# FFN input projections by Strassen's seven products on two of three token blocks, in a phase of their own

## The chip, the cores and the metric

The kernel runs on one core of a Trainium2 chip. The metric is the device time of one execution in microseconds (us). A profiled execution gives the trace from which all rows below are taken.

## The reference

The program is one step of a two-layer encoder over 1088 tokens (1024 of a new stream, 64 of a running one), with 1024 channels. Each layer is a mixer and a gated FFN, both behind an RMSNorm and with a residual sum. The change concerns the FFN alone:

```python
def conv_ffn(h, st, w_in, conv_w, conv_b, w_out):      # D_FF = 2816
    gu = h @ w_in
    g, u = gu[..., :D_FF], gu[..., D_FF:]
    g, new_st = causal_dwconv(g, conv_w, conv_b, st)   # width 3, along the tokens
    return (jax.nn.gelu(g) * u) @ w_out, new_st
# per layer: x = x + f, with f from conv_ffn(rmsnorm(x, norm_ffn[l]), ...)
```

## The kernel before

**Tiles.** Channels lie on the 128 partitions and tokens along the free axis: a tile is [128, T] with T = 1092, in three token blocks of BL = 364 (the text calls them blocks 0, 1 and 2). D_MODEL is KT = 8 such tiles, D_FF is FT = 22. Every fp32 operand is held as two fp32r parts h and l whose sum it is, and a product of a weight tile with an operand tile is three matmuls for each block: wh·xh, wl·xh and wh·xl (`product`, L167). One matmul has 128x128 weights and 364 columns. A projection of one output tile is thus 8 k-tiles x 3 terms x 3 blocks = 72 matmuls into one PSUM tile `pm` of three banks; the pool has two such tiles.

**Weights.** `weights` loads a [128, 1024] tile as two raw halves by SP's queue; ACT makes h by a copy (L131) and DVE makes l by a subtraction (L132).

**The FFN.** For each of the 22 tiles, `make` projects the gate (72 matmuls), multiplies it by 1/rms (L608), runs the conv (ACT L234, two DVE steps L236), GELU (ACT L611) and a product (L612); it then projects the up half (72 matmuls), multiplies it with the gate (L615), and splits the result into h and l in the pool `ring` (L186, L187). `chunks` runs the output product two k-tiles at a time, one step behind the making: `chunk` makes 8 output tiles of 18 matmuls each, and L260 adds each from PSUM to the residual sum XR, which stays in SBUF in eight slots of the pool `xr`. Input and output products alternate within the FFN.

**Before an FFN.** At the last chunk of the mixer's output product, `Next` makes the FFN's operands for each finished tile m: ACT L192 and DVE L193 scale and split it, and POOL adds its square to the sum for the norm (L202).

**What sets the order.** The Tile framework's scheduler orders each engine's instructions ahead of time by its own costs; on the chip each engine runs its list in that order, and waits at the first instruction whose semaphores are not there. Slots of a pool are reused in turn, so a new tile waits for the last reader of the tile before it.

Line numbers of this part are those of the kernel before; those named in the section on the change are of the changed one.

## Time and profile before

| what | value |
|---|---|
| three runs | 2795.62, 2793.54, 2795.61 us |
| median | 2795.61 us |
| span of the profiled execution | 2790.8 us |
| profiled execution beside the median | 4.8 us shorter |
| matmuls on PE | 16642, busy 98% of the span |
| DVE, ACT, POOL busy | 57%, 29%, 9% |

The span is the time from the first to the last instruction in the trace. Sums of durations are to be set against it, and the 4.8 us between it and the median of the three runs are carried along. The page shows shares of the whole span; the stretches show where one engine stands and another does not. PE stands for TensorE's matmuls, DVE for VectorE, ACT for ScalarE, POOL for GpSimd, and SP for the engine that issues most loads.

### The profile page before, as it was taken

The numbers are of one execution on the slowest core, as the hardware profiler recorded it, in microseconds if no ns is written. First come the engines' busy times: TensorE is split into PE (matmuls) and PEld (weight loads), VectorE is DVE, ScalarE is ACT, GpSimd is POOL, SyncE is SP. The second block draws the span as 40 slices with busy tenths as digits, with TensorE's granted clock in tenths as the row PEclk, the third lists the DMA queues.
The fourth block names the chain that finished last, engine by engine and source line by source line (L and its number), as shares of the span: only waits on it lengthen the run. The fifth ranks groups of instructions, "written<-read, shape, count | busy, mean of one in ns | idle before, by whom it ended". The sixth has DMA issues, their size and how long they took to land.

```text
span 2790.8 us, 39161 instructions
## 1 busy us (share of the span) xinstructions
PE 2745.5 (98%) x16642; PEld 2717.2 (97%) x16642; DVE 1601.7 (57%) x1723; ACT 803.4 (29%) x1083; POOL 242.8 (9%) x524
## 2 busy tenths in 40 slices
PE   8999999999999999999999999999999999999998
PEld 8999999999989999999999989999899999999997
DVE  7655665568675444444444587786744444444446
ACT  7323322232132222212212245551412112212223
POOL 1101111010030000000000030020300000000003
PEclk9999999999999999999999999999999999999999
DMA  3222332244211111111111121151111111111111
GB/s 131 78 82 81 99 97 82 86 127 138 66 43 41 46 46 46 42 46 42 46 46 45 64 82 58 55 199 53 38 46 46 42 46 45 42 46 42 42 47 68
DMA packets 83103, 183.02 MB, mean 66 GB/s; under 512 B 9808, under 2 KB 12416, under 8 KB 82928
## 3 DMA queue, kind: packets, MB, share of 16 engines
q1 hardware_dynamic: 67248, 123.40, 14.5%
q0 software_dynamic: 15392, 56.69, 6.1%
q8 instruction: 131, 2.15, 0.3%
...
## 4 chain that ended last, share of the span: by engine, by line
PE 94%; DVE 3%; issue 1%; ACT 1%; DMA 0%; POOL 0%; SPq 0%; DVEq 0%; ACTq 0%; POOLq 0%
PE pm L167 90%; DVE xg L193 1%; PE pa L507 1%; DVE xr L260 1%; PE pa L480 1%; PE pm L743 1%; DVE xg L772 0%; PE pa L518 0%; DVE wl L132 0%; PE pm L327 0%; PE pa L210 0%; PE pa L465 0%; DMA xr<-x 0%; DMA o_keep_lru<-keep_lru 0%; ACT xg L747 0%
## 5 line engine op out<-in xcount | busy, mean ns | idle before, releaser
L167 PE MATMUL pm<-xg,wh 128*128 128x364 f32 x7104 | 1406.8, 330 | 0.0
L167 PEld LDWEIGHTS pm<-xg,wh 128*128 128x128 f32 x7104 | 1204.6, 188 | 5.8 <-issue 2.6
L167 PE MATMUL pm<-xg,wl 128*128 128x364 f32 x3552 | 783.7, 328 | 0.0
L131 ACT ACTIVATE wh<-raw 128x512 fp32r<-128x512 f32 x440 | 274.8, 628 | 1481.7 <-PE pm L167 1259.8
L167 PE MATMUL pm<-ring,wh 128*128 128x364 f32 x3360 | 662.6, 331 | 22.3 <-DVE xr L260 17.2
L167 PEld LDWEIGHTS pm<-xg,wl 128*128 128x128 f32 x3552 | 619.9, 188 | 1.1
L167 PEld LDWEIGHTS pm<-ring,wh 128*128 128x128 f32 x3360 | 573.5, 189 | 27.4 <-DVE xr L260 20.2
L260 DVE TENSOR_TENSOR xr<-xr,pm 128x1092 f32<-128x1092 f32 x264 | 340.2, 1290 | 210.2 <-PE pm L167 204.4
L132 DVE TENSOR_TENSOR wl<-raw,wh 128x512 fp32r<-128x512 f32 x440 | 310.5, 708 | 243.8 <-ACT wh L131 243.6
L167 PE MATMUL pm<-ring,wl 128*128 128x364 f32 x1680 | 373.7, 331 | 0.0
L167 PEld LDWEIGHTS pm<-ring,wl 128*128 128x128 f32 x1680 | 295.4, 189 | 0.1
L226 POOL COPY wk<-par 128x2 f32<-128x2 f32 (+1 forms) x72 | 40.0, 555 | 1709.8 <-DVE wk L608 1416.2
L236 DVE SCALAR_TENSOR_TENSOR wk<-wk,par,wk 128x1092 f32<-128x1092 f32 x104 | 140.8, 1354 | 63.3 <-ACT wk L234 61.8
L608 DVE TENSOR_TENSOR wk<-pm,ss 128x1092 f32<-128x1092 f32 x44 | 57.0, 1295 | 193.0 <-PE pm L167 192.8
L615 DVE TENSOR_TENSOR wk<-pm,wk 128x1092 f32<-128x1092 f32 x44 | 57.0, 1295 | 119.7 <-PE pm L167 119.7
L187 DVE TENSOR_TENSOR ring<-wk,ring 128x1092 fp32r<-128x1092 f32 x68 | 87.9, 1294 | 36.5 <-ACT ring L186 32.8
L186 ACT ACTIVATE ring<-wk 128x1092 fp32r<-128x1092 f32 x68 | 75.7, 1116 | 100.0 <-PE pm L167 65.4
L612 DVE TENSOR_TENSOR wk<-wk,ss 128x1092 f32<-128x1092 f32 x44 | 57.0, 1296 | 52.1 <-ACT wk L611 52.1
L234 ACT ACTIVATE wk<-wk,par 128x1092 f32<-128x1092 f32 x52 | 67.7, 1302 | 65.5 <-POOL wk L226 65.3
L611 ACT ACTIVATE wk<-wk 128x1092 f32<-128x1092 f32 x44 | 49.2, 1118 | 121.2 <-DVE wk L236 121.2
L202 POOL TENSOR_TENSOR ss<-ss,wk 128x1092 f32<-128x1092 f32 x21 | 64.7, 3082 | 172.5 <-ACT wk L201 172.0
L193 DVE SCALAR_TENSOR_TENSOR xg<-xr,par,xg 128x1092 fp32r<-128x1092 f32 x32 | 64.5, 2024 | 11.8 <-ACT xg L192 11.5
...
## 6 DMA issues: line engine op xcount, KB each, us to landing
...
ring<-at_d POOLq DMA_DIRECT2D x16, 546.0 KB, 6.0
...
xr<-x SPq DMA_DIRECT2D x8, 546.0 KB, 7.3
...
```

Of the source, the lines that this page charges most:

```text
L131: S.activation(h, raw, AF.Copy)
L132: V.tensor_sub(l, raw, h.bitcast(F))
L167: TE.matmul(ps[:, b, 0:BL], w, x[:, b * BL:(b + 1) * BL], start=i == 0, stop=i == n - 1)
L186: S.activation(h, src, AF.Copy)
L187: V.tensor_sub(l, src, h.bitcast(F))
L193: split_last[0] = V.scalar_tensor_tensor(l, src, scale, h.bitcast(F), op0=OP.mult, op1=OP.subtract).ins
L202: by.tensor_add(ss, ss, sq)
L234: S.activation(out, cb[:, at:at + T], AF.Identity, bias=col(kind + "_b", i), scale=col(kind + "_w", i * w))
L236: V.scalar_tensor_tensor(out, cb[:, at + k:at + k + T], col(kind + "_w", i * w + k), out, op0=OP.mult, op1=OP.add)
L260: V.tensor_add(b3(XR[m]), b3(XR[m]), ps[:, :, 0:BL])
L608: V.tensor_mul(b3(cb[:, PAD:]), ps, b3(RS))
L612: V.tensor_mul(g, g, RS)
```

## The change

The gate and up projections are made for two output tiles at a time. The operand is a 2x2 block matrix: the two halves of the 8 k-tiles (k and k+4) by the token blocks 0 and 1. For these two blocks, `seven` makes seven products of half the depth in place of eight; block 2 is done plainly. Per pair of output tiles that is 7 x 12 + 2 x 24 = 132 matmuls, where before there were 2 x 72 = 144. One group is a pair's gate or a pair's up half: 22 groups in each layer.

`Pairs` takes the place of `Next` before an FFN. From each pair of residual tiles (m, m+4) it makes nine half-operands: `b11`, `b21`, `b22`, the combinations `t1` to `t4`, and `k0`, `k1` for the plain block. These fill 24 slots of `xg`. The order of the output tiles becomes 0, 4, 1, 5, 2, 6, 3, 7. `seven_weights` makes four weight operands from two raw tiles, among them two combinations: per group four ACT copies of 1024 columns (L348), four DVE subtractions of 1024 (L349) and four DVE steps of 512 (L353, L354, L357, L358). They fill the eight slots of `ring`.

In `seven`, `held` copies a product out of PSUM by ACT (L383), since it is needed by two sums or its bank is used again. `put` adds a held copy to a product (L740 in a gate group, L759 in an up group, 364 columns each), and at the second block multiplies 728 columns (L743 by 1/rms, L761 by the gate). `plain` evicts block 2 (L751, L765).

The results no longer go into the output product at once. Each is stored to DRAM (L762), all 22 groups of the layer come first, and then `chunks` reloads the tiles (L791) and splits them. `ring` is full of weights meanwhile, so the residual sum is also stored to DRAM and reloaded into `ring` (L710). All these transfers are issued by POOL. The pool `xg` has 24 slots instead of 16 and serves as `xr` as well; `raw` has two slots of 1024 columns instead of three of 512.

The core of the diff:

```diff
-    def xg(dt=R):
-        return slot("xg", 16, dt)
+    def xg(dt=R, cols=T):
+        return slot("xg", 24, dt, cols)
     def xr(dt=F, cols=T):
-        return slot("xr", 8, dt, cols)
+        return xg(dt, cols)
...
+    class Pairs(Next):
+        order = [m for k in range(HK) for m in (k, k + HK)]
+        def operands(self, m):
+            if m < HK:
+                return
+            x0, x1 = self.XR[m - HK], self.XR[m]
+            w0, w1 = col(self.key, m - HK), col(self.key, m)
+            ts, tu = wk(), wk()
+            u, t4 = tu[:, B[0]], tu[:, B[1]]
+            h, l = zip(*[(xg(), xg()) for _ in range(3)])
+            def scaled(i, b, n, x, w, at):
+                to = slice(b * BL, (b + n) * BL)
+                S.activation(h[i][:, to], x[:, at], AF.Copy, scale=w)
+                V.scalar_tensor_tensor(l[i][:, to], x[:, at], w, h[i][:, to].bitcast(F), op0=OP.mult, op1=OP.subtract)
+            S.activation(u, x0[:, B[0]], AF.Copy, scale=w0)
+            V.scalar_tensor_tensor(ts[:, B[0]], x0[:, B[1]], w0, u, op0=OP.mult, op1=OP.subtract)
+            V.scalar_tensor_tensor(ts[:, B[1]], x1[:, B[1]], w1, ts[:, B[0]], op0=OP.mult, op1=OP.subtract)
+            V.scalar_tensor_tensor(t4, x1[:, B[0]], w1, ts[:, B[1]], op0=OP.mult, op1=OP.subtract)
+            V.tensor_sub(ts[:, B[2]], ts[:, B[1]], u)
+            S.activation(h[2][:, B[0]], t4, AF.Copy)
+            V.tensor_sub(l[2][:, B[0]], t4, h[2][:, B[0]].bitcast(F))
+            scaled(2, 1, 1, x0, w0, B[2])
+            scaled(2, 2, 1, x1, w1, B[2])
+            S.activation(h[1], ts, AF.Copy)
+            V.tensor_sub(l[1], ts, h[1].bitcast(F))
+            scaled(0, 0, 1, x0, w0, B[0])
+            scaled(0, 1, 2, x1, w1, slice(0, 2 * BL))
+            self.xs.append((h, l))
+        def part(self, name, k):
+            i, b = PLACE[name]
+            h, l = self.xs[k]
+            return h[i][:, B[b]], l[i][:, B[b]]
+    def seven_weights(key0, key1):
...
+        out = []
+        raws = []
+        for key in (key0, key1):
+            n = n_of["w"] = n_of.get("w", 0) + 1
+            raw = wp.tile([P, 1024], F, tag="raw", bufs=2, name=f"raw{n}")
+            nc.sync.dma_start(raw, a[key[0]][key[1:]])
+            raws.append(raw)
+        r0, r1 = raws
+        lo, hi = slice(0, 512), slice(512, 1024)
+        def ready(raw):
+            h, l = ring(R, 1024), ring(R, 1024)
+            S.activation(h, raw, AF.Copy)
+            V.tensor_sub(l, raw, h.bitcast(F))
+            out.append((h, l))
+        ready(r1)
+        V.tensor_add(r1[:, hi], r1[:, lo], r1[:, hi])
+        V.tensor_sub(r1[:, lo], r0[:, lo], r1[:, lo])
+        ready(r1)
+        ready(r0)
+        V.tensor_sub(r0[:, lo], r1[:, hi], r0[:, lo])
+        V.tensor_sub(r0[:, hi], r0[:, hi], r0[:, lo])
+        ready(r0)
+        return out
...
+    def seven(ws, X, put, plain):
+        ta, tb = psum(), psum()
+        pw, pv1, pv0 = ta[:, 0, 0:BL], ta[:, 1, 0:BL], ta[:, 2, 0:BL]
+        px, py, pz = tb[:, 0, 0:BL], tb[:, 1, 0:BL], tb[:, 2, 0:BL]
+        def mul(ps, terms, first=True):
+            n = len(terms) * HK * 3
+            i = 0
+            for w, half, name in terms:
+                for k in range(HK):
+                    at = slice((half * HK + k) * P, (half * HK + k + 1) * P)
+                    wh, wl = w[0][:, at], w[1][:, at]
+                    xh, xl = X.part(name, k)
+                    for wx, x in ((wh, xh), (wl, xh), (wh, xl)):
+                        TE.matmul(ps, wx, x, start=first and i == 0, stop=i == n - 1, skip_group_check=True)
+                        i += 1
+        def held(ps):
+            n = n_of["cp"] = n_of.get("cp", 0) + 1
+            t = wp.tile([P, BL], F, tag="wh", bufs=6, name=f"cp{n}")
+            S.activation(t, ps, AF.Copy)
+            return t
+        a2, s31, a1, s24 = ws
+        mul(pw, [(a2, 1, "t4")])
+        mul(pv1, [(a2, 0, "k0"), (a2, 1, "k1")])
+        w = held(pw)
+        mul(pz, [(s31, 1, "t1")])
+        plain(1, pv1)
+        mul(px, [(a1, 0, "b11")])
+        p5 = held(pz)
+        mul(pv0, [(a1, 0, "k0"), (a1, 1, "k1")])
+        p1 = held(px)
+        mul(py, [(a1, 1, "b21")])
+        plain(0, pv0)
+        mul(px, [(s24, 0, "t2")], False)
+        put(0, 0, py, p1)
+        mul(pz, [(s24, 1, "b22")], False)
+        u2 = held(px)
+        mul(px, [(s31, 0, "t3")], False)
+        put(0, 1, pz, u2)
+        put(1, 0, px, w)
+        put(1, 1, px, p5)
...
+    def residual(src):
+        out = []
+        for m in Pairs.order:
+            t = ring()
+            nc.gpsimd.dma_start(t, src(m))
+            out.append((m, t))
+        return [t for _, t in sorted(out, key=lambda x: x[0])]
+    XR = residual(lambda m: a["x"][:, m])
...
-    def ffn(layer, XGs, rs, XR, done, after):
...
+        return split(y, xg)
+    def ffn(layer, X, done, after):
         kind = f"ffn{layer}"
+        h_d = scratch(f"h_d{layer}", [FT, P, T])
+        RS = X.rs()
+        two = slice(0, 2 * BL)
+        def gate(p):
+            cbs = [conv_buffer(), conv_buffer()]
+            gs = []
+            def put(m, b, ps, t):
+                V.tensor_add(cbs[m][:, PAD + b * BL:PAD + (b + 1) * BL], ps, t)
+                if b == 1:
+                    cb = cbs[m][:, PAD:]
+                    V.tensor_mul(cb[:, two], cb[:, two], RS[:, two])
+                    g = wk()
+                    conv(cbs[m], kind, 2 * p + m, g)
+                    S.activation(g, g, AF.Gelu_apprx_tanh)
+                    V.tensor_mul(g, g, RS)
+                    gs.append(g)
+            def plain(m, ps):
+                V.tensor_mul(cbs[m][:, PAD + 2 * BL:PAD + T], ps, RS[:, B[2]])
+            return put, plain, gs
+        def up(p, gs):
+            us = [wk(), wk()]
+            def put(m, b, ps, t):
+                V.tensor_add(us[m][:, B[b]], ps, t)
+                if b == 1:
+                    V.tensor_mul(us[m][:, two], us[m][:, two], gs[m][:, two])
+                    nc.gpsimd.dma_start(h_d[2 * p + m], us[m])
+            def plain(m, ps):
+                V.tensor_mul(us[m][:, B[2]], ps, gs[m][:, B[2]])
+            return put, plain
+        groups = [(p, u) for p in range(FT // 2) for u in range(2)]
+        def ready(g):
+            p, u = g
+            return seven_weights(*[("f_in", layer, 2 * (2 * p + m) + u) for m in range(2)])
+        ws = X.first
+        gs = None
+        for n, (p, u) in enumerate(groups):
+            nw = ready(groups[n + 1]) if n + 1 < len(groups) else None
+            if u == 0:
+                put, plain, gs = gate(p)
+            else:
+                put, plain = up(p, gs)
+            seven(ws, X, put, plain)
+            ws = nw
+        XR = residual(lambda m: X.spill[m])
+        done.XR = XR
+        def h_tile(f):
+            h = wk()
+            nc.gpsimd.dma_start(h, h_d[f])
+            return split(h, xg)
+        chunks(FT, h_tile, a["f_out"][layer], XR, done, after)
+        return XR
...
+    def first_weights(X, layer):
+        def make():
+            X.first = seven_weights(("f_in", layer, 0), ("f_in", layer, 2))
+        return make
+    nxt = Pairs(XR, "fn0", spill=scratch("xa_d", [KT, P, T]))
+    chunks(16, ab_tile, a["ab_out"], XR, nxt, first_weights(nxt, 0))
     x_d = scratch("x_d", [KT, P, T])
-    last, nxt = nxt, Next(XR, "mix1", spill=x_d)
-    ffn(0, last.xs, last.rs, XR, nxt, ("lru_in", 8))
-    # ---- layer 1's mixer
+    last, nxt = nxt, Next(None, "mix1", spill=x_d)
```

How the instructions stand on three engines, before and after, at the places that matter:

On ACT, in the first layer's FFN, before: weight halves (`wh`, L131) among the conv (L234), GELU (L611) and split (L186) of one tile.

```order
L234 ACTIVATE wk98_8047<-wk97_8045,par_75 128x1092
L611 ACTIVATE wk98_8047<-wk98_8047 128x1092
L131 ACTIVATE wh145_8337<-raw145_8336 128x512
L131 ACTIVATE wh146_8343<-raw146_8342 128x512
L186 ACTIVATE ring101_8144<-wk99_8142 128x1092
L131 ACTIVATE wh147_8349<-raw147_8348 128x512
```

The same place after, one up group: L236 and L746 are the conv and GELU of the two gate tiles `wk104` and `wk105`, `cp` are held copies of products, `ring` the next group's weights.

```order
L236 ACTIVATE wk104_7741<-wk102_7592,par_75 128x1092
L383 ACTIVATE cp13_7828<-pm116_7790 128x364
L236 ACTIVATE wk105_7754<-wk103_7593,par_75 128x1092
L348 ACTIVATE ring103_7768<-raw190_7766 128x1024
L746 ACTIVATE wk104_7741<-wk104_7741 128x1092
L383 ACTIVATE cp14_7855<-pm117_7791 128x364
L383 ACTIVATE cp15_7881<-pm117_7791 128x364
L746 ACTIVATE wk105_7754<-wk105_7754 128x1092
```

Two held copies of products of the up group (`cp14`, `cp15`) stand behind the first GELU of the gate group before it. On DVE the two gate tiles are finished in the same stretch; these are its rows there (`ss3` is 1/rms):

```order
L740 TENSOR_TENSOR wk102_7592<-pm115_7595,cp12_7725 128x364
L740 TENSOR_TENSOR wk103_7593<-pm115_7595,cp9_7632 128x364
L743 TENSOR_TENSOR wk102_7592<-wk102_7592,ss3_6899 128x728
L349 TENSOR_TENSOR ring102_7589<-raw187_7568,ring101_7588 128x1024
L740 TENSOR_TENSOR wk103_7593<-pm115_7595,cp10_7659 128x364
L238 SCALAR_TENSOR_TENSOR wk104_7741<-wk102_7592,par_75,wk104_7741 128x1092
L743 TENSOR_TENSOR wk103_7593<-wk103_7593,ss3_6899 128x728
L238 SCALAR_TENSOR_TENSOR wk104_7741<-wk102_7592,par_75,wk104_7741 128x1092
```

The first tile's conv (L238, `wk104`) now shares DVE with the eviction of the second tile and with a weight step, where before a gate tile's eviction was one instruction (L608).

On DVE before the first FFN, one pair's share, before: residual tiles `xr`, sums from PSUM (L260) and operands `xg` (L193).

```order
L260 TENSOR_TENSOR xr21_5502<-xr21_5502,pm106_7092 128x1092
L193 SCALAR_TENSOR_TENSOR xg24_7086<-xr20_5500,par_75,xg23_7085 128x1092
L193 SCALAR_TENSOR_TENSOR xg26_7113<-xr21_5502,par_75,xg25_7112 128x1092
L260 TENSOR_TENSOR xr22_5504<-xr22_5504,pm107_7119 128x1092
L260 TENSOR_TENSOR xr23_5506<-xr23_5506,pm108_7146 128x1092
```

After, the last pair's share, behind the last sum (L262); residual tiles are `ring` here, `t` operands `wk`:

```order
L262 TENSOR_TENSOR ring70_5420<-ring70_5420,pm109_7120 128x1092
L320 TENSOR_TENSOR xg82_7074<-wk88_7068,xg81_7073 128x364
L312 SCALAR_TENSOR_TENSOR xg82_7074<-ring67_5414,par_75,xg81_7073 128x364
L312 SCALAR_TENSOR_TENSOR xg82_7074<-ring68_5416,par_75,xg81_7073 128x364
L324 TENSOR_TENSOR xg80_7072<-wk87_7067,xg79_7071 128x1092
L312 SCALAR_TENSOR_TENSOR xg78_7070<-ring67_5414,par_75,xg77_7069 128x364
L312 SCALAR_TENSOR_TENSOR xg78_7070<-ring68_5416,par_75,xg77_7069 128x728
L315 SCALAR_TENSOR_TENSOR wk91_7140<-ring69_5418,par_75,wk92_7141 128x364
L316 SCALAR_TENSOR_TENSOR wk91_7140<-ring70_5420,par_75,wk91_7140 128x364
L349 TENSOR_TENSOR ring76_6869<-raw181_6854,ring75_6868 128x1024
```

Before, one operation of 1092 columns followed each sum; now ten smaller ones follow each pair of sums, with the weights' steps between them, and two pairs are still open when the last sum is made.

On POOL between the last group of the first FFN and its output product, after: `ring` from `xa_d` are reloads of the residual (L710), `h_d0` the FFN's results (L762 stores, L791 loads).

```order
L710 DMA ring252_11294<-xa_d_5422 128x1092
L710 DMA ring253_11296<-xa_d_5422 128x1092
L762 DMA h_d0_7170<-wk160_11130 128x1092
L762 DMA h_d0_7170<-wk161_11131 128x1092
L710 DMA ring254_11298<-xa_d_5422 128x1092
L791 DMA wk162_11300<-h_d0_7170 128x1092
L791 DMA wk163_11306<-h_d0_7170 128x1092
```

Before, POOL had at such a place only a conv's small copies:

```order
L225 MEMSET wk127_10845 128x4
L226 COPY wk127_10845<-par_75 128x2
L231 COPY keep_ffn0_88<-wk127_10845 128x2
L232 COPY keep_ffn0_88<-wk127_10845 128x2
L225 MEMSET wk130_11033 128x4
```

The loads of the first two tiles of the output product stand behind the two last stores and a reload.

## Rows read from the trace of the kernel before

**Rows 1.** The page: busy time by engine, and the chain by engine.
```profile
PE 2745.5 (98%) x16642; PEld 2717.2 (97%) x16642; DVE 1601.7 (57%) x1723; ACT 803.4 (29%) x1083; POOL 242.8 (9%) x524
...
PE 94%; DVE 3%; issue 1%; ACT 1%; DMA 0%; POOL 0%; SPq 0%; DVEq 0%; ACTq 0%; POOLq 0%
```

**Rows 2.** Busy time by stretch: us, PE, PEld, DVE, ACT, POOL, clock, DMA.
```profile
800.00:850.00 50.00, 44.31 (x248) 42.55 (x247) 41.87 (x35) 25.36 (x30) 22.31 (x12) 0.97 0.13 38
1000.00:1050.00 50.00, 50.00 (x302) 50.00 (x301) 23.51 (x22) 11.29 (x13) 1.72 (x8) 1.00 0.14 43
...
1950.00:2000.00 50.00, 44.29 (x248) 42.54 (x247) 41.24 (x33) 27.37 (x32) 22.87 (x12) 0.97 0.12 36
...
2700.00:2750.00 50.00, 50.00 (x302) 50.00 (x302) 24.13 (x23) 8.34 (x10) 1.40 (x4) 1.00 0.07 23
```

**Rows 3.** Groups by line and shape: count, busy us, mean ns, idle before.
```profile
L260 DVE TENSOR_TENSOR xr<-xr,pm 128x1092 f32<-128x1092 f32 x264 | 340.2, 1290 | 210.2 <-PE pm L167 204.4
L132 DVE TENSOR_TENSOR wl<-raw,wh 128x512 fp32r<-128x512 f32 x440 | 310.5, 708 | 243.8 <-ACT wh L131 243.6
...
L236 DVE SCALAR_TENSOR_TENSOR wk<-wk,par,wk 128x1092 f32<-128x1092 f32 x104 | 140.8, 1354 | 63.3 <-ACT wk L234 61.8
...
L186 ACT ACTIVATE ring<-wk 128x1092 fp32r<-128x1092 f32 x68 | 75.7, 1116 | 100.0 <-PE pm L167 65.4 <-DVE wk L615 31.5 <-PE pa L509 1.8
L234 ACT ACTIVATE wk<-wk,par 128x1092 f32<-128x1092 f32 x52 | 67.7, 1302 | 65.5 <-POOL wk L226 65.3
...
L455 DVE TENSOR_TENSOR ring<-ring,xr 128x1024 f32<-128x1024 f32 x16 | 19.5, 1222 | 3.8 <-ACT ring L453 3.7
...
L453 ACT ACTIVATE ring<-ring 128x1024 f32<-128x1024 f32 x16 | 16.7, 1047 | 0.0
...
L746 DVE TENSOR_TENSOR xr<-xr,pm 128x364 f32<-128x364 f32 x24 | 11.5, 525 | 8.6 <-PE pm L743 8.6
...
L747 ACT ACTIVATE xg<-xr 128x364 f32<-128x364 f32 x24 | 11.2, 506 | 23.2 <-DVE xr L746 23.2
```

**Rows 4.** Timeline of a hand-off in FFN 0: start, us, engine, line, operation.
```profile
1219.05 1.16 PE L167 MATMUL pm<-xg,wh 128*128 128x364 f32 x6
...
1219.75 1.30 DVE L608 TENSOR_TENSOR wk<-pm,ss 128x1092 f32<-128x1092 f32 x1 [4.58 <-PE pm L167]
```

**Rows 5.** Timeline of PE into FFN 0.
```profile
817.63 0.77 PE L167 MATMUL pm<-ring,wh 128*128 128x364 f32 x3 [4.00 <-DVE xr L260]
```

**Rows 6.** Timeline of DVE there.
```profile
796.02 1.36 DVE L193 SCALAR_TENSOR_TENSOR xg<-xr,par,xg 128x1092 fp32r<-128x1092 f32 x1 [1.28 <-ACT xg L192]
800.66 4.92 DVE L193 SCALAR_TENSOR_TENSOR xg<-xr,par,xg 128x1092 fp32r<-128x1092 f32 x2
810.23 6.14 DVE L193 SCALAR_TENSOR_TENSOR xg<-xr,par,xg 128x1092 fp32r<-128x1092 f32 x2
```

**Rows 7.** Timeline of POOL there.
```profile
800.92 7.04 POOL L202 TENSOR_TENSOR ss<-ss,wk 128x1092 f32<-128x1092 f32 x2 [80.98 <-ACT wk L201]
809.17 2.54 POOL L202 TENSOR_TENSOR ss<-ss,wk 128x1092 f32<-128x1092 f32 x1 [1.22 <-ACT wk L201]
812.70 2.52 POOL L202 TENSOR_TENSOR ss<-ss,wk 128x1092 f32<-128x1092 f32 x1 [0.99 <-ACT wk L201]
```

**Rows 8.** Busy time by stretch, columns as in Rows 2, around short gaps.
```profile
819.00:821.00 2.00, 2.00 (x9) 2.00 (x8) 1.25 (x2) 2.00 (x3) 1.04 (x1) 0.50 0.00 0
821.00:823.00 2.00, 2.00 (x10) 2.00 (x10) 2.00 (x1) 2.00 (x3) 1.92 (x2) 0.66 0.00 0
...
1618.00:1626.00 8.00, 7.62 (x29) 7.62 (x30) 7.18 (x6) 5.74 (x7) 6.31 (x4) 0.59 0.35 141
...
1795.00:1805.00 10.00, 7.08 (x43) 6.78 (x42) 5.47 (x5) 4.30 (x5) 2.83 (x12) 1.00 0.12 30
```

**Rows 9.** DMA issues: out<-in, queue, count, KB each, us to landing.
```profile
wk<-yz_d POOLq DMA_DIRECT2D x8, 546.0 KB, 4.0
...
wk<-hs_d POOLq DMA_DIRECT2D x8, 546.0 KB, 6.0
```

More of the change, by code (lines that the diff above doesn't have):

```diff
@@ L253, in softplus, with chunk @@
         V.scalar_tensor_tensor(x, x, 0.0, ln, op0=OP.max, op1=OP.add)
-    def chunk(xs, ws, XR, done=None):
-        for m in range(KT):
+    def chunk(xs, ws, XR, done=None, order=range(KT)):
+        for m in order:
             ps = psum()
@@ L268, in __init__ @@
             self.XR, self.key, self.xs, self.spill = XR, key, [], spill
+        order = range(KT)
+        def operands(self, m):
+            self.xs.append(split_scaled(self.XR[m], col(self.key, m), xg))
         def __call__(self, m):
-            self.xs.append(split_scaled(self.XR[m], col(self.key, m), xg))
+            self.operands(m)
             if self.spill is not None:
@@ L279, in rs, with operands @@
             return rms(self.ss, D)
+    HK = KT // 2
+    B = [slice(b * BL, (b + 1) * BL) for b in range(NB)]
+    PLACE = {"b11": (0, 0), "b21": (0, 1), "b22": (0, 2), "t1": (1, 0), "t2": (1, 1), "t3": (1, 2), "t4": (2, 0), "k0": (2, 1), "k1": (2, 2)}
+    class Pairs(Next):
+        order = [m for k in range(HK) for m in (k, k + HK)]
+        def operands(self, m):
+            if m < HK:
[27 more added lines that the diff above has]
+            return h[i][:, B[b]], l[i][:, B[b]]
@@ L287, in flush @@
             if i + 2 == n and after:
-                prefetch(after)
+                after()
             use = [tiles.pop(i), tiles.pop(i + 1)]
@@ L292, in flush @@
             else:
-                chunk(use, ws, XR, done if i + 2 == n else None)
+                chunk(use, ws, XR, *((done, done.order) if i + 2 == n else ()))
         for i in range(n):
@@ L575, in program @@
         short_conv(i, [group_prepare(1, *bc), now] if i == 3 else [now])
-    XR, RS2 = [], {}
-    for m in range(KT):
-        t = xr()
-        nc.gpsimd.dma_start(t, a["x"][:, m])
-        XR.append(t)
+    RS2 = {}
+    def residual(src):
[6 more added lines that the diff above has]
+    XR = residual(lambda m: a["x"][:, m])
     def ab_tile(i):
@@ L593, in ab_tile @@
             RS2[0] = rms(ssz[0], D)
-        return split(y, ring)
-    def ffn(layer, XGs, rs, XR, done, after):
+        return split(y, xg)
+    def ffn(layer, X, done, after):
         kind = f"ffn{layer}"
-        state = {}
-        def make(f):
-            ps = project(("f_in", layer, 2 * f), XGs)
-            if f == 0:
-                prefetch(("f_in", layer, 1))
-                state["rs"] = rs()
-            RS = state["rs"]
-            cb = conv_buffer()
-            V.tensor_mul(b3(cb[:, PAD:]), ps, b3(RS))
-            g = wk()
-            conv(cb, kind, f, g)
-            S.activation(g, g, AF.Gelu_apprx_tanh)
-            V.tensor_mul(g, g, RS)
-            ps = project(("f_in", layer, 2 * f + 1), XGs)
-            hh = wk()
-            V.tensor_mul(b3(hh), ps, b3(g))
-            return split(hh, ring)
-        chunks(FT, make, a["f_out"][layer], XR, done, after)
@@ L713, in program @@
         xb = nx
-    XR = []
-    for m in range(KT):
-        t = xr()
-        nc.gpsimd.dma_start(t, x_d[m])
-        XR.append(t)
+    XR = residual(lambda m: x_d[m])
     def c_tile(i):
@@ L722, in c_tile, with __call__, finish @@
         nc.gpsimd.dma_start(g, hs_d[i])
-        return split(g, ring)
-    nxt = Next(XR, "fn1")
-    chunks(8, c_tile, a["lru_out"], XR, nxt, ("f_in", 1, 0))
-    def finish(xs, ws):
+        return split(g, xg)
+    nxt = Pairs(XR, "fn1", spill=scratch("xb_d", [KT, P, T]))
+    chunks(8, c_tile, a["lru_out"], XR, nxt, first_weights(nxt, 1))
+    class Finish:
+        XR = None
+        def __call__(self, xs, ws):
+            finish(xs, ws, self.XR)
+    def finish(xs, ws, XR):
         ss = slot("ss", 2)
@@ L785, in finish @@
         results(2)
-    last = nxt
-    ffn(1, last.xs, last.rs, XR, finish, None)
+    ffn(1, nxt, Finish(), None)
     for k in keep:
```

15 lines of the change are left out of this document (8 added, 7 removed).

## The prediction

> **What bounds the kernel now.** I read the page's shares first. TensorE is busy for 2745.5 of 2790.8 us, and 94% of the chain that ends last is TensorE [rows 1]. That is an average, so I went by stretches: within the FFNs it is busy for all of 50 us at full clock with DVE at 23 to 24 us (from 1000 and from 2700) [rows 2], while in the stretches that lead into the two FFNs it stands for about 5.7 us of 50 with DVE busy for over 41 (from 800 and from 1950) [rows 2]. So an FFN is bound by the number of matmuls, with slack on DVE and ACT, and a transition into it by DVE. The change takes matmuls away where the first holds, and adds work where the second does. What decides is whether the slack lies where the new waits fall.
>
> 50 us show 302 matmuls with those cut at the edges, so 300 whole ones of 0.1667 us each; the stretch at 2700, in which six matmuls in a row go to one PSUM bank as they will in a product of the seven, shows the same [rows 2]. A reader of PSUM starts 0.2 us after the last matmul's slot (six from 1219.05 end their slots at 1220.05, of which the first three belong to the finished tile, whose slot ends at 1219.55; L608 starts at 1219.75) [rows 4].
>
> **Term 1, matmuls.** A pair of tiles takes 132 instead of 144; there are 11 pairs x 2 halves x 2 layers = 44 groups, so 528 go: 528 x 0.1667 = **-88.0 us**.
>
> **Term 2, new waits in the groups.** Work first. Per gate and up pair DVE gets 8 x 1.22 (L349, as L455) + 8 x 0.71 (as L132) + 12 x 0.525 (364 columns from PSUM, as L746) + 4 x 0.91 (728 columns, between L746 and L260: (0.525 + 1.290)/2) + 4 x 1.354 (conv) + 2 x 1.29 = 33.4 us, ACT about 17 [rows 3]. TensorE has 264 x 0.1667 = 44.0 us, where it had 48.0. So by sums TensorE still bounds; the waits come from order.
>
> I followed the up group's chain through the order shown. Let E be the end of the gate group's last product. DVE: 0.2 us, two L740 (0.525 each), L743 (0.91): E+2.1. ACT's conv step, as L234, 1.30: E+3.4. DVE meanwhile does L349 (1.22) and L740: E+3.8, which TensorE meets with its 22 remaining matmuls (3.7 us): 0.1 us lost. DVE then L238 (1.354) to 5.1, L743 to 6.0, L238 to 7.2 (some 0.1 less in all, since DVE's instructions follow each other closely). ACT's second conv runs 6.0 to 7.2, and L348 (1.05, as L453) stands in front of GELU (1.12, as L186): 9.3. Only then come the two held copies (0.506 each, as L747): E+10.2. TensorE has two products of 12 in that time: E+3.7+4.0 = 7.7. Its third waits for the second copy: **2.5 us**. It runs 24 more (to 14.2), and needs a bank that L765 frees. On DVE that is behind L238, L349, L747, L238, two 512-column steps, and, after the second GELU, L747 again: 7.1 + 1.35 + 1.22 + 1.29 + 1.35 + 1.42 = 13.7, GELU lies beside the last two, then 1.29 + 0.525: about E+15.4, **1.1 us**. In both halves smaller waits of 0.15 us stand at the second additions to a held bank: **0.4 us**. I add 0.1 for the 0.1 above: 4.1 us. The order repeats in every pair, so 22 x 4.1 = **+90 us**. A pair then takes 48.1 us against 48.0 before.
>
> Bounds: each of the four 364-column ACT or DVE steps, the pairs of conv steps and the two GELUs has a row, so I allow 1.5 us per pair up and 2 down (DVE steps that overlap at their ends): +46 to +123. Stalls of 2.5 us have a second price only if they lower the clock. It stood at 1.00 after a stretch with TensorE 2.9 us idle, and fell to 0.50 after one gap of 4.0 [rows 5, 8]; I take no fall here.
>
> **Term 3, into the FFNs.** Let the last chunk's first product start at 0; TensorE has 8 x 18 x 0.1667 = 24.0 us. DVE: first sum at 3.2, a gap of 1.7 before the second of the pair, then eight sums x 1.29, 4 pairs x 6.6 (ten steps: six of 364 at 0.55, two at 0.53, 1.29, 0.95), three L349, four 512-column steps, less 3.9 that stands behind what the first product needs: 3.2 + 1.7 + 10.3 + 26.4 + 3.7 + 2.8 - 3.9 = 44.2. TensorE waits 20 us. Beside it POOL adds squares, and DVE is slower then: two L193 took 4.92 and two 6.14, where one alone takes 1.36 [rows 6, 7]; that is 5.6 us for four adds, 1.4 each, with 7 adds in each transition: 10. The first PSUM evictions then wait for 1/rms, some 2 us. Half clock behind so long a gap costs 1.7, as behind the 4.0 of before (2 us at 0.50, then 2 at 0.66) [rows 5, 8]. That is 34, of which before has 9 already (302 less 248 matmuls x 0.1667) [rows 2]: **+25 each, +50 us**. Bounds: without any effect of POOL +15; with every add blocking DVE for its whole 2.5 us [rows 7], 17.5 us instead of 10, +33. So +30 to +66.
>
> On this price the trace says more: the two L193 at 800.66 took 2.2 us more than two alone, and the two adds beside them 7.04 us, 2.0 more than two of 2.54; each lost about one step of the other engine [rows 6, 7].
>
> The Trainium skill, "SBUF — State Buffer", section "Who interferes with whom", says that the port pair which VectorE and GpSimd share is locked for a whole instruction when the VectorE step has two SBUF inputs and GpSimd reads SBUF. By that rule each add that meets such a step blocks it for its full length, and the term would be the +66 of the upper bound; the trace agrees with a lock, but four adds cost 5.6 us and not 10, so not every add met such a step.
>
> **Term 4, out of the input phase.** There was none: input and output products alternated. Now the first h tiles come from DRAM. DVE: two L759 and L761 give the first store at E+2.1, L759, a weight step and L761 the second at E+4.0. Both stores and a reload stand on POOL's queue ahead of the first load. A 546 KB load takes 4.0 to 6.0 us to land [rows 9], ACT's split 1.12 and the start of DVE's 0.2: TensorE goes on at E+9.5 to E+12. Half clock behind the gap costs 1.7 us, as above, to 3.3 (8 us at 0.59) [rows 8]. I take 11 + 2.5 = **13.5 each, +27 us**; the bounds are 8 and 20 (the reloads of the residual share the DMA engines with these loads): +16 to +40.
>
> **Term 5, elsewhere.** The residual is loaded into `ring` behind the mixer's tail, some +2 us, 0 to +5. Slots: `xg` has eight more, and `wl` one less, which nothing in the FFN waits for.
>
> **Sum.** 2790.8 - 88.0 + 90 + 50 + 27 + 2 = 2872 us of span; with the 4.8 us to the median, **2877 us**, 2.9% slower. All lower bounds give 2790.8 - 88 + 46 + 30 + 16 + 0 + 4.8 = 2800; all upper 2790.8 - 88 + 123 + 66 + 40 + 5 + 4.8 = 2942.
>
> **Rivals.**
> *Bound by matmuls after all.* If the held copies reach ACT in time (another order of arrival than I followed, steps that overlap more), the waits in a group vanish, TensorE stays as full as in [rows 2], and -88 stands against transitions of lower price: 2790.8 - 88 + 10 (0.45 us in each pair) + 30 + 16 + 4.8 = 2764, faster. For it: DVE has 33 us of work in 44, ACT 17. Against: both engines work in order and the copy stands behind two GELUs' chain. It decides from waits below (88 - 79)/22 = 0.4 us per pair with the other terms as I take them, or below (88 - 46)/22 = 1.9 with these at their lower bounds.
> *Half clock in each up group.* The gap of 2.5 us is close to that of 4.0 which brought 0.50 [rows 5, 8], and 1.7 us is the price: 22 x 1.7 = 37, so 2914. Against: the stretch at 1795 at 1.00 [rows 8].
> *Transitions at their upper ends.* DVE blocked by every add and loads slowed by the reloads: 66 - 50 + 40 - 27 = 29 more, 2906.
> *It doesn't save what it says:* were the matmuls of one bank slower for the dependence of each on the last, the 88 would shrink; the stretch from 2700 [rows 2] speaks against it.
>
> **Chances.** Forecast (2840 to 2895) 0.50, half clock 0.12, transitions at the upper end 0.15, waits at their lower bounds but still slower (2801 to 2840) 0.08, bound by matmuls 0.13, the last 0.02. Below 2790 lie about 0.12, above 2930 about 0.05, so the range is 2790 to 2930. A difference under 0.2% (5.6 us) is about what a measurement of this kernel can't tell from none: 2790 to 2801, 0.02. Faster 0.13, slower 0.85.
>
> **What would show it.** Matmuls: 16114 in the program instead of 16642. In a stretch of an input phase: TensorE at about 91% (44.0/48.1), with its largest idle put down to ACT's L383 before an up group's third product, 2 to 3 us long, and a second to DVE L765. DVE over 65% there. Into each FFN 25 to 35 us of idle TensorE in all behind DVE's L312 and L320. Between input and output product one gap of 9 to 12 us, behind a load of an h tile, with the clock at half behind it. I am wrong if stretches of the input phase show TensorE full (the first rival), or if their granted clock lies below 1.00 (the second).

## The result: 3.8% slower, and the profile after

The changed kernel took 2899.38 us (median of four runs, 2898.45 to 2903.19); the kernel before took 2795.12 us beside it (four runs). The ratio is 1.0376, with a 95% interval of 1.0361 to 1.0391. The forecast was 2877 us in a range of 2790 to 2930. The profiled execution has a span of 2901.4 us, 110.6 more than before. The medians lie only 104.3 us apart: the profiled execution of the changed kernel is the slowest of its four, 3.8 us above their median.

The page of the kernel after, busy us by engine:

```profile
PE 2713.2 (94%) x16114; PEld 2651.1 (91%) x16114; DVE 1933.1 (67%) x2227; ACT 965.0 (33%) x1300; POOL 284.0 (10%) x644
```

Against [rows 1] TensorE has 528 matmuls less, as the diff says, and yet its busy share fell from 98% to 94%: the span grew around it. Its busy time fell by only 32 us, not by 88. Part of the difference is the granted clock, whose mean was 0.996 before and is 0.977 now; that mean counts stretches in which TensorE stands too, so it does not say how large a part.

Three groups of the same page (busy, mean ns; idle before, and what ended it):

```profile
L383 ACT ACTIVATE cp<-pm 128x364 f32<-128x364 f32 x176 | 77.4, 465 | 100.3 <-PE pm L377 100.3
L765 DVE TENSOR_TENSOR wk<-pm,wk 128x364 f32<-128x364 f32 x44 | 23.6, 537 | 83.5 <-PE pm L377 82.7
...
wk<-h_d POOLq DMA_DIRECT2D x44, 546.0 KB, 5.0
```

The held copy takes 0.465 us (0.506 in [rows 3] for the same shape) and the 364-column eviction 0.537 (0.525 there): the single steps cost what the nearest rows said.

**An input phase.** Busy time by stretch, columns as in [rows 2], of an input phase, then TensorE's timeline over one whole pair in the first FFN:

```profile
1050.00:1100.00 50.00, 46.96 (x278) 45.70 (x277) 31.73 (x38) 16.22 (x20) 2.14 (x10) 1.00 0.20 65
```

```profile
949.64 43.91 PE L377 MATMUL pm<-xg,ring 128*128 128x364 f32 x256
995.46 4.24 PE L377 MATMUL pm<-xg,ring 128*128 128x364 f32 x24 [1.90 <-ACT cp L383]
1000.83 40.74 PE L377 MATMUL pm<-xg,ring 128*128 128x364 f32 x240 [1.14 <-DVE wk L765]
```

From one wait to the same wait of the next pair TensorE does 24 and 240 matmuls, the 264 of a pair. It stops twice, 24 matmuls apart, and in this pair no granted clock is lost by it (1.00, as in the stretch above). ACT's timeline ahead of the first stop:

```profile
991.37 1.30 ACT L236 ACTIVATE wk<-wk,par 128x1092 f32<-128x1092 f32 x1 [1.45 <-DVE wk L743]
992.61 1.06 ACT L348 ACTIVATE ring<-raw 128x1024 fp32r<-128x1024 f32 x1
993.58 1.10 ACT L746 ACTIVATE wk<-wk 128x1092 f32<-128x1092 f32 x1
994.58 0.82 ACT L383 ACTIVATE cp<-pm 128x364 f32<-128x364 f32 x2
```

The gate group's last product ended at E = 985.66, which is 0.2 us before DVE's L740 begins to read it at 985.86. The second gate tile's conv runs, then a weight copy, then GELU, and only behind these the two held copies: they end at 995.40, E+9.7, and TensorE goes on at 995.46. The waits of TensorE over most of the input phase (us in total, times, longest) show that this repeats from pair to pair:

```profile
PE pm L377 <- ACT cp L383: 14.7, 8, 1.9
PE pm L377 <- DVE wk L765: 9.5, 8, 1.2
```

The granted clock did not stay at 1.00 behind every such stop. Behind six of the 22 (at 899 and 947 in the first FFN, at 2104, 2152, 2200 and 2248 in the second) it fell to half. One of these stretches, and TensorE over another of these pairs:

```profile
947.00:951.00 4.00, 3.68 (x13) 3.68 (x14) 3.96 (x6) 1.38 (x2) 0.10 (x1) 0.58 0.00 0
```

```profile
2151.93 46.20 PE L377 MATMUL pm<-xg,ring 128*128 128x364 f32 x264 [1.84 <-ACT cp L383]
```

In that pair the second stop does not appear, and the pair is as long as the others (48.0 us).

**Into the first FFN.** By stretch, then TensorE, DVE and POOL by timeline:

```profile
800.00:850.00 50.00, 36.67 (x193) 35.17 (x191) 42.57 (x38) 20.52 (x27) 19.91 (x13) 0.90 0.23 90
850.00:900.00 50.00, 38.63 (x196) 35.49 (x197) 42.06 (x55) 26.40 (x36) 5.37 (x12) 0.90 0.16 54
```

```profile
836.90 1.28 PE L169 MATMUL pm<-xg,wh 128*128 128x364 f32 x3 [5.98 <-DVE ring L262]
...
861.11 2.79 PE L212 MATMUL pa<-ss,ones 128*128 128x364 f32 x4 [5.37 <-POOL ss L204]
```

```profile
829.77 2.84 DVE L316 SCALAR_TENSOR_TENSOR wk<-ring,par,wk 128x364 f32<-128x364 f32 x1
832.54 0.68 DVE L354 TENSOR_TENSOR raw<-raw,raw 128x512 f32<-128x512 f32 x1
833.14 0.58 DVE L317 SCALAR_TENSOR_TENSOR wk<-ring,par,wk 128x364 f32<-128x364 f32 x1
```

```profile
829.40 2.82 POOL L204 TENSOR_TENSOR ss<-ss,wk 128x1092 f32<-128x1092 f32 x1 [0.93 <-ACT wk L203]
```

The first stretch held 248 matmuls in [rows 2] and holds 193 now; the second holds 196 where a full one holds some 300. DVE's step L316 takes 2.84 us beside POOL's add and ends 0.4 us after it; L317, of the same form, takes 0.58 alone. A blocked step thus costs some 2.3 us, nearly the whole add, where the four adds of [rows 6, 7] had cost 1.4 each.

**Out of the input phase.** TensorE, POOL's queue, and the transfers issued in the gap (queue, count, KB each, us to landing):

```profile
1390.53 2.27 PE L377 MATMUL pm<-xg,ring 128*128 128x364 f32 x12 [0.61 <-ACT cp L383]
1408.40 1.28 PE L169 MATMUL pm<-xg,wh 128*128 128x364 f32 x3 [15.60 <-ACT xg L188]
```

```profile
1396.81 0.54 POOL L762 DMA_DIRECT2D h_d<-wk  x1 [1.34 <-DVE wk L761]
1397.33 0.54 POOL L710 DMA_DIRECT2D ring<-xa_d  x1
1397.86 1.57 POOL L791 DMA_DIRECT2D wk<-h_d  x3
```

```profile
wk<-h_d POOLq DMA_DIRECT2D x3, 546.0 KB, 10.2
```

```profile
1392.00:1408.00 16.00, 0.80 (x5) 0.49 (x3) 5.20 (x9) 2.58 (x5) 4.74 (x9) 0.59 1.01 386
1408.00:1412.00 4.00, 3.60 (x12) 3.60 (x13) 3.50 (x3) 3.27 (x4) 1.05 (x2) 0.52 0.96 368
```

TensorE is idle for 15.6 us (17.9 in the second FFN) and then runs at a granted clock of 0.52. The loads that end the gap take 10.2 us to land, where the median load of `h_d` takes 5.0; by the last two columns of the stretch, the DMA engines are full (1.01) meanwhile, with the residual's reloads and the stores beside these loads.

**The start.** SP's issues in the first 30 us, in the kernel before and then after, and TensorE after:

```profile
3.45 1.03 SPq L130 DMA_DIRECT2D raw<-ab_in  x2
6.01 2.80 SPq L307 DMA_DIRECT2D xr<-x  x5
```

```profile
...
8.54 2.00 SPq L127 DMA_DIRECT2D raw<-ab_in  x2
10.59 0.42 SPq L433 DMA_DIRECT2D xg<-x  x1
14.87 0.33 SPq L127 DMA_DIRECT2D raw<-ab_in  x1
15.25 0.90 SPq L433 DMA_DIRECT2D xg<-x  x2
26.66 0.33 SPq L127 DMA_DIRECT2D raw<-ab_in  x1
27.04 1.38 SPq L433 DMA_DIRECT2D xg<-x  x3
```

```profile
32.96 1.15 PE L453 MATMUL pm<-xg,w_dt 128*48 128x364 f32 x3 [3.21 <-ACT xg L194]
```

Before, all tiles of x were issued by 8.8 us. Now the weight loads take turns with them on SP's queue, each waiting for one of the two `raw` slots (three before), and the last three tiles of x go out at 27.04.

**Where the 110.6 us came from**, by the lag of matching matmuls behind the kernel before, in the two profiled executions (6.3 us more than between the medians):

| part | matmuls | waits | net, us |
|---|---|---|---|
| first 45 us of the start | | | +13.6 |
| rest of mixer 0, and its output projection | | | +3.0 |
| FFN 0 | -44.0 | pairs +43.4, way in +25.2, way out +17.3 | +41.9 |
| FFN 0 to the mixer of layer 1 | | | +3.9 |
| that mixer and its output projection | | | +4.3 |
| FFN 1 and the end | -44.0 | pairs +43.4, way in +24.4, way out some +20 | +43.8 |

A pair takes 48.0 us in both FFNs, as long as the 144 + 144 matmuls of before. The first pair of the first FFN, which has the end of the way in within it, takes 66.9.

### The profile page after: what moved, and what is told of

The parts are those of the page before. It is cut to its first block, busy times and chain, and to the rows that moved or that the text cites. A ratio compares the mean times of both kernels' runs of the same rounds, so it can differ in the third digit from the quotient of the medians.

```text
span 2901.4 us, 38693 instructions
## 1 busy us (share of the span) xinstructions
PE 2713.2 (94%) x16114; PEld 2651.1 (91%) x16114; DVE 1933.1 (67%) x2227; ACT 965.0 (33%) x1300; POOL 284.0 (10%) x644
## 5 line engine op out<-in xcount | busy, mean ns | idle before, releaser
L169 PE MATMUL pm<-xg,wh 128*128 128x364 f32 x6048 | 1217.0, 333 | 69.8 <-ACT xg L188 33.5
L169 PEld LDWEIGHTS pm<-xg,wh 128*128 128x128 f32 x6048 | 1037.9, 190 | 82.1 <-DVE ring L262 36.1
L377 PE MATMUL pm<-xg,ring 128*128 128x364 f32 x5808 | 1005.8, 334 | 72.3 <-ACT cp L383 44.6
L377 PEld LDWEIGHTS pm<-xg,ring 128*128 128x128 f32 x5808 | 975.5, 190 | 102.0 <-ACT cp L383 55.4
L169 PE MATMUL pm<-xg,wl 128*128 128x364 f32 x3024 | 674.7, 331 | 0.0
L262 DVE TENSOR_TENSOR ring<-ring,pm 128x1092 f32<-128x1092 f32 x264 | 340.1, 1289 | 244.2 <-PE pm L169 237.2
L133 ACT ACTIVATE wh<-raw 128x512 fp32r<-128x512 f32 x264 | 163.6, 628 | 835.8 <-PE pm L169 806.6
L349 DVE TENSOR_TENSOR ring<-raw,ring 128x1024 fp32r<-128x1024 f32 x176 | 215.2, 1223 | 207.7 <-ACT ring L348 207.6
L348 ACT ACTIVATE ring<-raw 128x1024 fp32r<-128x1024 f32 x176 | 186.4, 1059 | 495.3 <-PE pm L377 342.8
L134 DVE TENSOR_TENSOR wl<-raw,wh 128x512 fp32r<-128x512 f32 x264 | 180.5, 687 | 153.6 <-PE pm L169 92.4
L238 DVE SCALAR_TENSOR_TENSOR wk<-wk,par,wk 128x1092 f32<-128x1092 f32 x104 | 140.5, 1351 | 4.0 <-ACT wk L236 0.4
L383 ACT ACTIVATE cp<-pm 128x364 f32<-128x364 f32 x176 | 77.4, 465 | 100.3 <-PE pm L377 100.3
L236 ACT ACTIVATE wk<-wk,par 128x1092 f32<-128x1092 f32 x52 | 67.8, 1303 | 58.8 <-DVE wk L743 50.0
L765 DVE TENSOR_TENSOR wk<-pm,wk 128x364 f32<-128x364 f32 x44 | 23.6, 537 | 83.5 <-PE pm L377 82.7
L746 ACT ACTIVATE wk<-wk 128x1092 f32<-128x1092 f32 x44 | 48.8, 1109 | 46.7 <-DVE wk L238 46.7
L762 POOL DMA_DIRECT2D h_d<-wk x44 | 23.5, 534 | 353.7 <-DVE wk L761 348.9
```

Of the source, the lines that this page charges most:

```text
L133: S.activation(h, raw, AF.Copy)
L134: V.tensor_sub(l, raw, h.bitcast(F))
L169: TE.matmul(ps[:, b, 0:BL], w, x[:, b * BL:(b + 1) * BL], start=i == 0, stop=i == n - 1)
L236: S.activation(out, cb[:, at:at + T], AF.Identity, bias=col(kind + "_b", i), scale=col(kind + "_w", i * w))
L238: V.scalar_tensor_tensor(out, cb[:, at + k:at + k + T], col(kind + "_w", i * w + k), out, op0=OP.mult, op1=OP.add)
L262: V.tensor_add(b3(XR[m]), b3(XR[m]), ps[:, :, 0:BL])
```

## Experiments

The ratios are to the kernel before; differences in us are between medians, to the 2899.4 of the kernel after where no other is named.

**Order of the products.** In the order in which TensorE runs an up group, the product `py` into bank 1 of the PSUM tile `tb` stands at the first stop. The copy for which it waits, `held(px)`, reads bank 0 of that tile. At the second stop `pv0` is to go into bank 2 of `ta`, and waits for L765, which reads `pv1` in bank 1. So both wait for readers of another bank of the same tile. The edit puts `pv0`, a product into the other tile, between `held(px)` and `py`, moves `plain(1, pv1)` behind `pv0`, and puts `pw` late:

```diff
-        mul(pw, [(a2, 1, "t4")])
         mul(pv1, [(a2, 0, "k0"), (a2, 1, "k1")])
-        w = held(pw)
         mul(pz, [(s31, 1, "t1")])
-        plain(1, pv1)
         mul(px, [(a1, 0, "b11")])
         p5 = held(pz)
-        mul(pv0, [(a1, 0, "k0"), (a1, 1, "k1")])
         p1 = held(px)
+        mul(pv0, [(a1, 0, "k0"), (a1, 1, "k1")])
+        plain(1, pv1)
+        plain(0, pv0)
         mul(py, [(a1, 1, "b21")])
-        plain(0, pv0)
         mul(px, [(s24, 0, "t2")], False)
-        put(0, 0, py, p1)
         mul(pz, [(s24, 1, "b22")], False)
         u2 = held(px)
+        mul(pw, [(a2, 1, "t4")])
+        w = held(pw)
         mul(px, [(s31, 0, "t3")], False)
+        put(0, 0, py, p1)
         put(0, 1, pz, u2)
```

> The seven products are written in another order, so that every copy or eviction out of a PSUM tile is followed by at least 12 matmuls into the other tile before the next product goes into the same tile; the work is the same. Theory: the waits in the groups (4.0 us of each 48.0 us pair) come from two products that wait for readers of another bank of their tile, which stand behind the GELU chain on ACT and DVE. Then a pair takes 44.0 to 44.5 us and the time falls by 22 x 3.5 to 4.0, to 2812 to 2823 us. Rival, ACT and DVE too full for 44 us: the wait moves to another product, a pair stays above 47 us, and the time stays above 2875.

Measured: 2811.55 us, ratio 1.0063 (1.0048 to 1.0078), 87.8 us less, at the end of what was expected. The same view of this kernel's input phase, and TensorE's timeline there:

```profile
1000.00:1050.00 50.00, 50.00 (x300) 49.60 (x300) 32.89 (x41) 16.73 (x22) 2.79 (x12) 1.00 0.29 98
```

```profile
998.82 52.43 PE L377 MATMUL pm<-xg,ring 128*128 128x364 f32 x312
```

The view shows no stop of TensorE over 312 matmuls, a pair takes 44.3 us, and DVE is busy for 32.89 of 50 us. So ACT and DVE were not too full. The order alone cost 3.7 us in each of the later pairs, and 84.8 us in the two input phases together, of the 87.8. That the order causes the two waits is shown. That they were for another bank is read from the program: the rows name the tile and not the bank, and no run changes the bank alone.

**Earlier loads of h.** The edit puts the first load ahead of the last group and two more ahead of the residual's reloads:

```diff
+        loads = {}
+        def load(f):
+            h = wk()
+            nc.gpsimd.dma_start(h, h_d[f])
+            return h
...
+            if n == len(groups) - 1:
+                loads[0] = load(0)
             seven(ws, X, put, plain)
...
+        loads[1] = load(1)
+        loads[2] = load(2)
         XR = residual(lambda m: X.spill[m])
...
-            h = wk()
-            nc.gpsimd.dma_start(h, h_d[f])
-            return split(h, xg)
+            return split(loads.pop(f) if f in loads else load(f), xg)
```

> The loads of the first three tiles of results are issued ahead of the reload of the residual, the first of them during the last group. Theory: the gaps of 15.6 and 17.9 us between input and output product come from these loads standing behind stores and reloads. Then each gap falls below 6 us, and the time falls by 20 to 26, to 2873 to 2879. Rival, the round trip of the results through DRAM and the split take that long by themselves: gaps of 12 or more, and 2890 or more.

Measured: 2868.96 us, ratio 1.0263 (1.0246 to 1.028), 30.4 us less, more than expected. TensorE at the place of the 15.6 us:

```profile
1388.04 2.27 PE L377 MATMUL pm<-xg,ring 128*128 128x364 f32 x12 [0.61 <-ACT cp L383]
1390.15 0.66 PE L169 MATMUL pm<-xg,wh 128*128 128x364 f32 x3
...
1392.31 0.77 PE L169 MATMUL pm<-xg,wh 128*128 128x364 f32 x3 [0.50 <-ACT xg L188]
```

The gap is gone in the first FFN (0.5 left) and is 4.2 us in the second. By the lag, the first FFN is 14.9 us shorter and the second 14.0. So the round trip through DRAM does not cost the gap by itself; it came from when the loads are issued. Issued earlier, they also no longer run beside all the reloads, and the run does not separate the two.

**POOL's adds left out.** The squares of seven of the eight tiles are left out of the norm's sum ahead of both FFNs and of the second mixer:

```diff
-            sum_square(self.ss, self.XR[m], m == 0, G)
+            if m == 0:
+                sum_square(self.ss, self.XR[m], True, G)
```

> Left out: the sums of squares of seven of the eight tiles before both FFNs and before the second mixer (the norms then use the first tile alone), that is ACT's squares and POOL's adds. Theory: POOL's adds slow DVE in the transitions, 1.4 us each, and hold up 1/rms; without them each transition into an FFN is 12 to 17 us shorter and the one into the mixer 3 to 5, together 27 to 39: 2860 to 2872. Rival, DVE's own added work alone sets the transitions: less than 12 us in all, above 2887.

Measured: 2857.75 us, ratio 1.0226 (1.021 to 1.0241), 41.6 us less: 17 on the way into FFN 0, 13.6 into the second mixer, 11.5 into FFN 1. The stretch behind the hand-over:

```profile
850.00:900.00 50.00, 45.81 (x265) 44.32 (x264) 36.40 (x49) 19.53 (x24) 0.95 (x7) 0.98 0.14 42
```

TensorE does 265 matmuls there instead of 196. This bounds what the adds and the squares on ACT cost together; where the work of the adds is best done is tried below.

**Tiles of x by another queue.** Two runs ask whether SP's queue at the start is what costs 13.6 us. The first loads x by POOL's queue:

```diff
-        nc.sync.dma_start(t, a["x"][:, k])
+        nc.gpsimd.dma_start(t, a["x"][:, k])
```

> Only the eight loads of x at the start move from SP's queue to POOL's. Theory: the changed kernel loses 13.6 us in its first 45 us because loads of x stand on SP's queue behind weight loads that wait for one of now two raw slots. Then x arrives as it did before, and the time falls by 10 to 14 us, to 2885 to 2889. Rival, the weight loads of 512 KB delay x on the DMA engines themselves: within 4 us of 2899.

Measured: 2898.07 us, ratio 1.0371 (1.0356 to 1.0387), within the 4 us that the rival was given. The lag after the start fell from 13.6 to 9.6 us, less than a cause on SP's queue alone would give, and not by much more than chance: in the three runs above that leave the start alone, it was 12.8, 10.9 and 13.2. The second leaves x on SP and ties the first two weight tiles to the last of DVE's split steps of x:

```diff
-    prefetch((w_in, 0))
-    prefetch((w_in, 1))
+    with tc.issue_after(split_last[0]):
+        prefetch((w_in, 0))
+        prefetch((w_in, 1))
```

> In the changed kernel the first weights of the second and third projection are converted only after the last tile of x has been split, so most loads of x are issued ahead of their loads. Moving x to another queue gave 4 of the 13.6 us lost at the start back, and ACT still had weight copies, which wait for slots that matmuls free, ahead of the scaling of x. Theory: that order is the rest; the start then loses under 6 us and the time falls by 8 to 13, to 2886 to 2892. Rival, loads of 512 KB take the DMA engines from x: again 9 us or more are lost at the start, above 2894.

Measured: 2898.19 us, ratio 1.0372 (1.0356 to 1.0387), again the rival's time, and a lag of 9.7. The edge held DVE's part of the prefetch only. SP, and ACT in this kernel:

```profile
8.50 2.00 SPq L127 DMA_DIRECT2D raw<-ab_in  x2
10.55 4.03 SPq L433 DMA_DIRECT2D xg<-x  x6
```

```profile
25.04 0.63 ACT L133 ACTIVATE wh<-raw 128x512 fp32r<-128x512 f32 x1 [3.71 <-PE pm L169]
25.57 1.19 ACT L194 ACTIVATE xg<-xg,par 128x1092 fp32r<-128x1092 f32 x1
```

Two weight loads still go first, and on ACT a weight copy waits 3.71 us for a slot that TensorE holds, with the scaling of x behind it. So neither run puts x first on both SP and ACT; the next one does.

**Both at once.** The prefetch is tied to the last load of x on SP and the last scaling on ACT:

```diff
+        x_last = nc.sync.dma_start(t, a["x"][:, k]).ins
...
+    x_split = split_last[1]
...
-    prefetch((w_in, 0))
-    prefetch((w_in, 1))
+    with tc.issue_after(x_last), tc.issue_after(x_split):
+        prefetch((w_in, 0))
+        prefetch((w_in, 1))
```

> The changed kernel with the weights of the second and third projection held back on both SP and ACT until all tiles of x are loaded and scaled (the earlier edit held back only DVE's part of them: SP still issued two weight loads ahead of six tiles, and ACT still waited 3.7 us for a slot in front of the fifth tile). Theory: the order on these two queues is the cause of the 13.6 us at the start. Then under 4 us are lost there, and the time falls by 9 to 13, to 2886 to 2890. Rival, the 512 KB pieces themselves: 8 us or more lost at the start, above 2893.

Measured: 2893.5 us, ratio 1.0351 (1.0334 to 1.0368); the lag after the start is 3.8 us and the span 9.6 shorter, the median 5.9, which is less than the 9 to 13 expected. SP and TensorE:

```profile
2.12 5.71 SPq L433 DMA_DIRECT2D xg<-x  x7
8.59 47.70 SPq L127 DMA_DIRECT2D raw<-ab_in  x6
```

```profile
32.97 1.09 PE L169 MATMUL pm<-xg,wh 128*128 128x364 f32 x3 [1.98 <-DVE ring L457]
```

The lag is well below those of the other runs, so the order of the first loads and copies is most of what is lost at the start: about 10 of the 13.6 us between the profiled executions, 5.9 by the medians. Of the rest 2 us is the wait shown.

**Do the three costs add up?** The new order of products, the earlier loads and the DVE edge on the prefetch in one kernel:

> The three edits together: the other order of the seven products, the early loads of results, and x ahead of weights. If the costs lie one behind the other on TensorE they add: 2899.4 - 87.8 - 30.4 - 10 = 2771, which is below the kernel before (2794). Rival, they overlap (a wait removed in one place comes back in the next): above 2790.

Measured: 2783.84 us (seven runs), ratio 0.9965 (0.9953 to 0.9976). That is 115.5 us less, where the three runs alone give 87.8 + 30.4 + 1.2 = 119.4: they add up to within 4 us. The 2771 expected had counted 10 us for the start. With this the change is no longer a loss, though the gain is small; the ways into the FFNs are left.

**Where the squares are added.** In that kernel the adds go to DVE, all of them or only the last of each half:

```diff
-            sum_square(self.ss, self.XR[m], m == 0, G)
+            sum_square(self.ss, self.XR[m], m == 0, V)
```

> As the three edits together, and all sums of squares before the FFNs and the second mixer added on DVE instead of POOL. Leaving the sums out gave 41.6 us in three transitions. Theory, POOL's adds cost by running against DVE and by being last: DVE pays 7 x 1.29 = 9 us in each of three transitions and gains 14, so 10 to 18 us less than with the three edits. Rival, the cost of the sums is the work itself, wherever it stands: within 6 us of the three edits, or slower.

Measured: 2764.06 us, ratio 0.9895 (0.988 to 0.9909), 19.8 less than with the adds on POOL and somewhat more than expected.

```diff
+            sum_square(self.ss, self.XR[m], m == 0, V if m % HK == HK - 1 else G)
```

> As the three edits together, and only the sums of the last two tiles (3 and 7) added on DVE, the others on POOL. Theory as for all on DVE, but with two adds: 1/rms no longer waits for POOL's last two adds (5 us at each transition), DVE pays 2.6: 6 to 12 us less than with the three edits. Rival: within 4 us.

Measured: 2777.36 us, ratio 0.9938 (0.9923 to 0.9953), 6.5 less. TensorE where 1/rms is needed, in the kernel with three edits and then with all adds on DVE; and the stretches from 800 and 850 in the same order:

```profile
853.98 2.79 PE L212 MATMUL pa<-ss,ones 128*128 128x364 f32 x4 [4.67 <-POOL ss L204]
```

```profile
853.16 1.39 PE L212 MATMUL pa<-ss,ones 128*128 128x364 f32 x4
```

```profile
800.00:850.00 50.00, 33.63 (x164) 31.60 (x162) 46.40 (x45) 25.89 (x35) 20.79 (x14) 0.84 0.25 100
850.00:900.00 50.00, 45.15 (x250) 42.62 (x250) 39.48 (x51) 23.19 (x32) 4.49 (x10) 0.92 0.14 43
```

```profile
800.00:850.00 50.00, 35.01 (x170) 33.32 (x169) 45.62 (x59) 28.04 (x38) 4.36 (x9) 0.82 0.29 111
850.00:900.00 50.00, 48.87 (x281) 47.49 (x280) 39.43 (x52) 22.65 (x31) 1.60 (x10) 0.98 0.13 43
```

With the adds on DVE the wait of 4.67 us is gone and DVE is not busier, neither where most of the adds lie (45.62 against 46.40) nor behind (39.43 against 39.48): the steps that it took over cost it no more than the stretched ones had.

**The best version.** All adds on DVE, the order, the loads, and the start of the run with both edges:

> All that helped, together: the other order of the seven products, early loads of results, sums of squares on DVE, and x ahead of weights on SP and ACT. Without the last it was 2764. Theory: 4 to 6 us less, since 6 us were still lost at the start there: 2758 to 2761, 1.2% below the kernel before. Rival: the start is bound by the arrival of x, 2764 as before.

Measured: 2764.05 us, ratio 0.9888 (0.9874 to 0.9903), the same as without the better start (2764.06). The lag there was 4.8 instead of 6.1 us, and as little came through. This version is 1.1% faster than the kernel before. How much of that is due to Strassen's products is not shown: the kernel before adds its squares on POOL as well, and the adds on DVE were not tried in it. The three edits that only mend what the change brought give 0.35%.

## Why the prediction was right, and where a term was off

The direction and its reason held: the matmuls saved are given back as waits by in-order engines. By the steps of the prediction, in us of span:

| term | predicted | measured | what the runs show |
|---|---|---|---|
| 1, matmuls | -88 | -88 | 16114 matmuls, 528 less, at 0.1667 us: a count, not a time measured by itself |
| 2, waits in the groups | +90 | +87 | pair of 48.0, not 48.1; -87.8 with another order |
| 3, into the FFNs | +50 | +50 | 25.2 and 24.4 |
| 4, out of the input phase | +27 | some +37 | 17.3 and some 20 |
| 5, elsewhere | +2 | +25 | start 13.6, 3.0, 3.9, 4.3 |

The measured terms are parts of the lag in the table above; they sum to its 110.6 but for rounding.

**Term 2** was followed instruction by instruction, and that is why it holds: the copies were put at E+10.2 and ended at E+9.7; the stop at the copy was to be 2.5 us and is 1.9, that at L765 was to be 1.1 and is 1.14 here, and 0.9 rather than 0.5 us lies in smaller waits. The rival that the waits vanish fell. That of the half clock was half right in its mechanism: the granted clock fell behind six of the 22 stops, and stayed at 1.00 behind the others. It was wrong in its price, since the pairs with it are no longer than those without (48.0 us). What sets these six apart stays open. But the prediction took the order for a given. It named the GELU chain as the cause; a reordering of six lines, with the chain and the copies still there, removes the cost.

**Term 3** came out in its sum with a different split. I had 10 us for POOL's adds and most of the rest for DVE's own work. By the 2.3 us of a blocked step seven adds cost some 16, near the 17.5 of my upper bound. Leaving them out, with ACT's squares, gave 17 and 11.5. DVE's own work would then be less than I worked out; it was not measured by itself. Nor do the waits bear the names that I had given: between 815 and 900, TensorE waited 10.6 us for L262, 5.4 for POOL's last add and 4.1 for ACT's L319, and not for L312 and L320. The price of 1.4 us from [rows 6, 7] was read where DVE had long steps with gaps; in the changed kernel DVE goes from one short step to the next, and nearly every add meets one. So "with every add blocking DVE" was the better value. That the sum still came out is luck: one error covered the other.

**Term 4** is one mis-sized item. The landing of 4.0 to 6.0 us was taken from loads that go alone [rows 9], and in the gap they share the DMA engines with stores and reloads: 10.2 us. TensorE goes on at E+15.8, not at E+9.5 to E+12. The bound of 20 each, which named that sharing, holds both gaps.

**Term 5** is the step of the prediction that failed: "Slots: `xg` has eight more, and `wl` one less, which nothing in the FFN waits for." That may be so in the FFN, but I looked at the FFN only. The first 45 us of the program, far from the change, lost 13.6 us, most of it by the order in which loads and copies now stand there; whether the two `raw` slots instead of three made that order was not tried. The reload of the residual, at 2, was all that I had priced. Term 5's 23 us more are most of the 29 us by which the span exceeds my 2872; by the medians the forecast was 22 us too low.

Open stays what the last 2 to 4 us of the start are, why an earlier start in the best version bought nothing, and the 3.9 and 4.3 us around the second mixer, of which the adds explain a part (in the kernel with three edits, putting them on DVE turned 3.8 into -4.2).
